# Delta rule: one sweep of nine steps for four heads, with copies over eight matrices, in place of two sweeps for two heads each

## The chip, the cores and the metric

The kernel runs on one core of a Trainium2 chip, in fp32. The metric is the device time of one execution in microseconds. Within the core TensorE does the matrix products, VectorE and ScalarE the elementwise work, GpSimd issues some of the transfers, and SyncE the weight loads. Each engine works through its own list of instructions in order; the order of each list is fixed when the kernel is built.

## The reference

One layer of a bidirectional hybrid block, for 256 tokens of width 2048:

```
mod  = silu(c) @ W_ada + b_ada          # six vectors: shift, scale, gate, twice
h    = RMSNorm(x) * (1 + scale) + shift
proj = h @ W_in                         # columns for the branches below
A    = bidirectional mLSTM, 4 heads (q, k 256 wide, v 512 wide)
B    = bidirectional gated delta rule, 16 heads of 128 (conv of 5 taps, SiLU, then the rule)
x    = x + gate * ((g_a * (A @ W_a) + g_b * (B @ W_b)) @ W_out)
x    = x + gate * SwiGLU(RMSNorm(x) * (1 + scale) + shift)
out  = RMSNorm(x)
```

The delta rule of one head and direction is S_t = a_t (I - b_t k_t k_t^T) S_{t-1} + b_t k_t v_t^T with o_t = S_t^T q_t. In chunks it needs the inverse T of a unit triangular matrix A = I + strict(b K K^T decay). With T known, a chunk takes a few products: T applied to the values, the correction between chunks, T applied again, and the output.

## The kernel before

**Products.** Weights come from memory in 1 MB tiles `raw`, are split by ScalarE into a high half (`wh`, a rounded copy) and by VectorE into a low half (`wl`, the remainder), and are multiplied in three products: high by high, high by low, low by high. `fjob` (L172 to L192) does one 128-column block of the input projection in two pieces of 24 matmuls of 256 columns; `tjob` (L198 to L274) does 512 columns in eight pieces of 12 matmuls of 512 columns. Both are generators: each `next` traces one piece. The tags `wh`, `wl` and `raw` have three buffers each.

**Filling.** `fills` is the list of projection jobs whose results go to memory for later: values, output gates, queries and keys of the mLSTM, merge gates. `fill(n)` traces n pieces of it. What is left of the list when the delta rule ends is emptied by `fill(1)`, `fill(2)` and `fill(1000)` at L1195 to L1205, among the first steps of the mLSTM.

**The delta rule.** The sixteen heads go in four groups of four (`GRP`). For a group:

- `gdn_phase1` (L639) prepares a head in two parts: decay matrices, the products of keys and queries, the matrices `cc`, `gg`, `at`, the values `vv` and the small factors `sm`. `gg`, `at`, `vv` and `cc` have six buffers (`NB`), so up to six heads are alive at once.
- `gdn_invert` (L747) inverts all 32 x 32 blocks of the four heads on VectorE, and `gdn_blocks` (L782) lays the inverses into `R`, `X` and `UL`.
- `gdn_phase2(g, p)` (L810), for p = 0 and 1, solves two heads, that is four matrices (two chunks by two heads), in nine steps. Steps 1 to 4 join the blocks to 64 and then 128 (matmuls `p1` to `p4` at L822, L831, L844, L856, with masked copies to `pt` at L823 and L845, a transposition at L834, and ScalarE copies to `X` and `UL`). Step 5 applies the inverse (`pa`), step 6 corrects between chunks (`pb`, `r` at L881), step 7 applies it again (`pc`), step 8 makes the output (`po`, L890 to L895) and squares it in `gdn_norm`, and step 9 scales it, transposes it (`px`, L902) and stores it (`obt`, L906 and L907).

**The order around it.** The loop at L1095 runs `gdn_phase2` step by step, and after step n traces `after[n]` (second pair `second[n]`, last group `last[n]`) pieces of `stream` (L948): first the projection jobs of two heads of the next group (twelve pieces, with the parts of `gdn_phase1` two and four pieces behind each head), then fills. A pair so gets 16 pieces in groups 0 to 2, that is 12 of the heads and 4 fills, and 13 fills in group 3.

**The modulation rows.** The matrix W_ada of the later four vectors is used row by row: `ask` loads one row tile of 1 MB and `add` (L120, the instruction at L125) multiplies it with silu(c) and sums it on VectorE. 48 rows are wanted before the feed-forward part, where `affn` (L1441) is made of them. `pump`, called once in each piece, asks for a row and adds it:

```
        if every[0] and count[0] % every[0] == 0:
            owed[0] = 1
        more = bool(unasked and every[0] and homes)
        if asked and owed[0] and asked[0][-1] > 2 and not held[0]:
            owed[0] = 0
            add()
        if more:
            ask()
```

There is one tile (`homes`) for a row until L1228, and two from there to L1440. `every` is 1 in the delta steps, 0 in the inversions and from L1192 to L1221, and 3 from L1229. `held` is true in steps 1 to 3 of each sweep, and no row is added then. At the fourth piece of the last output projection, L1437 to L1439, `sums` adds what is left.

**Order of the lists.** A planner orders each engine's list by the order of tracing and by when it expects inputs and buffers to be there. `order(...)` keeps an instruction behind the one traced before it on its engine, but does not hold later work back.

Of the kernel before, what the change touches and what calls it, by code (L numbers as in the profile page):

```python
# [15 lines left out]
P = 128  # L16
T = 256
# [35 lines left out]
def hybrid_block(ctx: ExitStack, tc: tile.TileContext, xr, nfr, crow, pk_d, cst_d, ada2, ada4, win0, winb, wint, wba, wbb, wo, wgu, wd, out, dbg=None):  # L53
# [693 lines left out]
    def gdn_invert(g):  # L747

        uu = uus.pop(g)
        tmp = bk.tile([64, 256], F32, tag="utmp", bufs=1, name=f"utmp{g}")  # L750
        cg = cgs[g] = bk.tile([P, 2, 4, P], F32, tag="z", bufs=1, name=f"cg{g}").rearrange("p k m c -> p k (m c)")
# [58 lines left out]
    def gdn_phase2(g, p):  # L810

        hd = [heads.pop(4 * g + 2 * p + e) for e in range(2)]
        te = [(t, e) for t in range(2) for e in range(2)]
        hs = slice(2 * p, 2 * p + 2)
        X4 = X.rearrange("p k (t h) q c -> p k t h q c", t=2)
        UL4 = UL.rearrange("p k (t h) c -> p k t h c", t=2)
        m4 = lambda a: a.rearrange("p (t h c) -> p t h c", t=2, h=2)

        p1 = gps(f"p1_{g}_{p}")
        pt0 = bk.tile([P, 4, P], F32, tag="pt", bufs=2, name=f"pt0_{g}_{p}")  # L820
        for i, (t, e) in enumerate(te):
            PE.matmul(p1[:, i * 32 : (i + 1) * 32], hd[e][0][:, 0, t], R[:, 0, 4 * t + 2 * p + e], start=True, stop=True)  # L822
        V.tensor_tensor(  # L823
            pt0.rearrange("p m (b c) -> p m b c", b=4),
            p1[:, 0:P].rearrange("p (m c) -> p m c", m=4).unsqueeze(2).broadcast_to([P, 4, 4, 32]),
            nxt.unsqueeze(1).unsqueeze(3).broadcast_to([P, 4, 4, 32]), ALU.mult,
        )
        yield
        p2 = gps(f"p2_{g}_{p}")
        for i, (t, e) in enumerate(te):  # L830
            PE.matmul(p2[:, i * 32 : (i + 1) * 32], pt0[:, i], R[:, 1, 4 * t + 2 * p + e], start=True, stop=True)  # L831
        E_ = p2[:, 0:P]
        Et = bk.tile([P, P], F32, tag="Et", bufs=1, name=f"Et{g}_{p}")
        V.transpose(Et, E_)  # L834
        S.activation(X4[32:64, 1, :, hs, 0], m4(E_[32:64]), AF.Copy)
        S.activation(X4[64:96, 1, :, hs, 1], m4(E_[64:96]), AF.Copy)
        S.activation(X4[32:64, 0, :, hs, 0], m4(Et[0:32]), AF.Copy)
        S.activation(X4[64:96, 0, :, hs, 1], m4(Et[96:128]), AF.Copy)
        yield

        p3 = gps(f"p3_{g}_{p}")
        pt1 = bk.tile([P, 4, P], F32, tag="pt", bufs=2, name=f"pt1_{g}_{p}")
        for i, (t, e) in enumerate(te):
            PE.matmul(p3[:, i * 64 : (i + 1) * 64], hd[e][0][:, 1, t], X[:, 0, 4 * t + 2 * p + e], start=True, stop=True)  # L844
        V.tensor_tensor(  # L845
            pt1.rearrange("p m (b c) -> p m b c", b=2),
            p3[:, 0 : 2 * P].rearrange("p (m c) -> p m c", m=4).unsqueeze(2).broadcast_to([P, 4, 2, 64]),
            half.unsqueeze(1).unsqueeze(3).broadcast_to([P, 4, 2, 64]), ALU.mult,
        )
        for b in range(4):  # L850
            c = 32 * (b ^ 1)
            S.activation(UL4[32 * b : 32 * b + 32, b % 2, :, hs, c : c + 32], m4(E_[32 * b : 32 * b + 32]), AF.Copy)
        yield
        p4 = gps(f"p4_{g}_{p}")
        for i, (t, e) in enumerate(te):
            PE.matmul(p4[:, i * 64 : (i + 1) * 64], pt1[:, i], X[:, 1, 4 * t + 2 * p + e], start=True, stop=True)  # L856
        S.activation(UL4[0:64, 0, :, hs, 64:128], m4(p4[0:64, 0 : 2 * P]), AF.Copy)
        V.tensor_copy(UL4[64:128, 1, :, hs, 0:64], m4(p4[64:128, 0 : 2 * P]))
        yield

        z = bk.tile([P, 2, 4, P], F32, tag="z", bufs=1, name=f"z{g}_{p}")
        r = bk.tile([P, 2, 2, P], F32, tag="r", bufs=1, name=f"r{g}_{p}")
        pair4 = lambda ps: ps.rearrange("p (e k c) -> p e k c", e=2, k=2)

        def apply(name, rhs, t0, t1):
            ps = pair4(gps(f"{name}_{g}_{p}"))
            for e in range(2):
                PE.matmul(ps[:, e, 0], UL4[:, 0, t0, 2 * p + e], rhs(e)[:, 0], start=True, stop=True)
                PE.matmul(ps[:, e, 1], UL4[:, 1, t1, 2 * p + e], rhs(e)[:, 1], start=True, stop=True)
            for e in range(2):  # L870
                sg3 = hd[e][5]
                S.activation(z[:, e, t0], ps[:, e, 0], AF.Copy, scale=sg3[:, t0, 0:1])
                S.activation(z[:, e, 2 + t1], ps[:, e, 1], AF.Copy, scale=sg3[:, t1, 1:2])

        apply("pa", lambda e: hd[e][3], 0, 1)
        yield
        pb = pair4(gps(f"pb_{g}_{p}"))
        for e in range(2):
            for i in range(2):
                PE.matmul(pb[:, e, i], hd[e][1][:, i], z[:, e, 3 * i], start=True, stop=True)  # L880
            V.tensor_tensor(r[:, e], hd[e][3][:, ::-1], pb[:, e], ALU.subtract)  # L881
        yield
        apply("pc", lambda e: r[:, e], 1, 0)
        yield
        po2 = gps(f"po_{g}_{p}")
        px = gps(f"px_{g}_{p}")
        for e in range(2):
            at, zz_ = hd[e][2], z[:, e]
# [10 lines left out]
        for e, on in enumerate(ons):  # L899
            h, hl_ = 4 * g + 2 * p + e, 2 * p + e  # L900
            for t in range(2):
                PE.transpose(px[:, (2 * e + t) * P : (2 * e + t + 1) * P], on[:, t], ident)  # L902
# [787 lines left out]
```

## Time and profile before

| what | value |
|---|---|
| median of three runs | 1951.5 us (1947.19 to 1954.09) |
| the profiled execution | 1949.33 us |
| its span, first to last instruction | 1947.5 us |
| TensorE busy (matmul) | 1919.7 us, 99% |
| VectorE busy | 1406.7 us, 72% |
| ScalarE busy | 1033.8 us, 53% |
| mean of the 16 DMA engines' traffic | 249 GB/s |
| four delta stages with both sweeps (groups 0 to 3) | 116.05, 115.39, 115.20, 90.70 us |

The profile names engines PE (matmul), PEld (weight load of TensorE), DVE (VectorE), ACT (ScalarE), POOL (GpSimd) and SP (SyncE). A row `p<-R,cc 128x32 f32 x8` is a group of instructions that write `p` from `R` and `cc`. An fp32 matmul appears as two records.

### The profile page before, as it was taken

What the parts mean: (1) busy time and instruction counts of PE and PEld (TensorE: products, weight loads), DVE (VectorE), ACT (ScalarE), POOL (GpSimd) and SP (SyncE); (2) the same over time, 40 slices, a digit from 0 to 9 for tenths busy, and PEclk for the clock granted to TensorE, in tenths of its full rate; (3) what the DMA queues carried; (4) which work ended last, traced back from release to release, by engine and by line L of the source; (5) the groups of instructions that cost most, each with busy time, mean ns of one, the idle gap of its engine ahead of it and who ended that gap; (6) DMA issues with size and microseconds to landing.
All of it is one profiled execution on the core that took longest, in us unless ns stands there. A gap on an engine that the chain in (4) does not pass through costs nothing.

```text
span 1947.5 us, 27217 instructions
## 1 busy us (share of the span) xinstructions
PE 1919.7 (99%) x10436; PEld 1699.3 (87%) x10436; DVE 1406.7 (72%) x2084; ACT 1033.8 (53%) x1564; POOL 124.1 (6%) x223
## 2 busy tenths in 40 slices
PE   8999999999999999999999999999999999999997
PEld 6888889998999899889788888888888888888886
DVE  6788886898788789876577988766666565555554
ACT  3147656775776587565544444644444444444443
POOL 0001220111011101120100000200000000000000
PEclk9999999999999999999999999999999999999999
DMA  9997676667676766686777998576667665655563
GB/s 399 420 358 236 188 256 249 214 224 238 219 220 204 241 220 238 208 293 245 268 289 266 351 353 314 195 263 245 246 239 260 239 219 199 204 207 209 196 208 137
DMA packets 80774, 485.68 MB, mean 249 GB/s; under 512 B 11434, under 2 KB 17138, under 8 KB 26626
## 3 DMA queue, kind: packets, MB, share of 16 engines
q1 hardware_dynamic: 64368, 451.02, 63.9%
q0 software_dynamic: 8672, 17.88, 4.3%
q10 hardware_dynamic: 7602, 15.03, 2.0%
q8 instruction: 82, 1.34, 0.3%
q14 instruction: 50, 0.40, 0.1%
HBM read 467.07 MB, written 16.82 MB: 248 GB/s over the span
## 4 chain that ended last, share of the span: by engine, by line
PE 90%; DMA 4%; DVE 3%; ACT 2%; issue 1%; SPq 0%; DVEq 0%; ACTq 0%
PE acc_up L247 4%; PE acc_up L249 4%; PE acc_up L248 4%; PE acc_gt L248 4%; PE acc_d L248 4%; PE acc_gt L249 4%; PE acc_d L247 4%; PE acc_d L249 4%; PE acc_gt L247 4%; DMA ra<-ada 3%; PE acc_b L186 3%; PE acc_o L247 3%; PE acc_o L248 3%; PE acc_o L249 3%; PE acc_b L188 3%; PE acc_b L187 3%
## 5 line engine op out<-in xcount | busy, mean ns | idle before, releaser
L215 DVE TENSOR_TENSOR wl_d<-raw_d,wh_d 128x1024 fp32r<-128x1024 f32 x88 | 107.7, 1225 | 105.9 <-ACT wh_d L213 105.9
L215 DVE TENSOR_TENSOR wl_up<-raw_up,wh_up 128x1024 fp32r<-128x1024 f32 x88 | 107.7, 1225 | 100.7 <-ACT wh_up L213 100.7
L215 DVE TENSOR_TENSOR wl_gt<-raw_gt,wh_gt 128x1024 fp32r<-128x1024 f32 x88 | 107.7, 1224 | 78.6 <-ACT wh_gt L213 78.6
L186 PE MATMUL acc_b<-hh,wh_b 128*128 128x256 f32 x576 | 161.9, 281 | 0.0
L213 ACT ACTIVATE wh_d<-raw_d 128x1024 fp32r<-128x1024 f32 x88 | 92.9, 1056 | 126.5 <-PE acc_d L248 117.7
L188 PE MATMUL acc_b<-hh,wl_b 128*128 128x256 f32 x576 | 158.7, 276 | 0.0
L187 PE MATMUL acc_b<-hl,wh_b 128*128 128x256 f32 x576 | 158.3, 275 | 0.0
L213 ACT ACTIVATE wh_gt<-raw_gt 128x1024 fp32r<-128x1024 f32 x88 | 92.8, 1055 | 117.1 <-PE acc_gt L248 71.1
L213 ACT ACTIVATE wh_up<-raw_up 128x1024 fp32r<-128x1024 f32 x88 | 92.7, 1055 | 108.1 <-PE acc_up L248 77.1
L125 DVE SCALAR_TENSOR_TENSOR ada<-ada,crow 128x2048 f32<-128x2048 f32 x64 | 146.2, 2284 | 0.0
L247 PE MATMUL acc_up<-wh_up,hfh 128*128 128x512 f32 x352 | 133.4, 379 | 0.0
L248 PE MATMUL acc_up<-wh_up,hfl 128*128 128x512 f32 x352 | 133.4, 379 | 0.0
L249 PE MATMUL acc_up<-wl_up,hfh 128*128 128x512 f32 x352 | 133.4, 379 | 0.0
L247 PE MATMUL acc_gt<-wh_gt,hfh 128*128 128x512 f32 x344 | 131.6, 383 | 0.0
L248 PE MATMUL acc_gt<-wh_gt,hfl 128*128 128x512 f32 x344 | 131.3, 382 | 0.2 <-DVE hfl L1475 0.2
L247 PE MATMUL acc_d<-wh_d,ffh 128*128 128x512 f32 x344 | 130.5, 379 | 0.0
L248 PE MATMUL acc_d<-wh_d,ffl 128*128 128x512 f32 x344 | 130.5, 379 | 0.0
L249 PE MATMUL acc_gt<-wl_gt,hfh 128*128 128x512 f32 x344 | 130.4, 379 | 0.0
L249 PE MATMUL acc_d<-wl_d,ffh 128*128 128x512 f32 x344 | 130.4, 379 | 0.0
L595 PE MATMUL first<-x,raw 128*128 128x256 f32 x488 | 110.1, 386 | 6.0 <-ACT x L587 6.0
L595 PEld LDWEIGHTS first<-x,raw 128*128 128x128 f32 x488 | 92.9, 192 | 23.3 <-ACT x L587 10.7
L187 PEld LDWEIGHTS acc_b<-hl,wh_b 128*128 128x128 f32 x576 | 110.6, 192 | 0.1
(403 smaller groups left out, 5294.7 us busy)
## 6 DMA issues: line engine op xcount, KB each, us to landing
ada<-ada SPq DMA_DIRECT2D x64, 1024.0 KB, 5.2
raw_gt<-wgu SPq DMA_DIRECT2D x44, 1024.0 KB, 5.0
raw_up<-wgu SPq DMA_DIRECT2D x44, 1024.0 KB, 5.0
raw_d<-wd SPq DMA_DIRECT2D x44, 1024.0 KB, 4.9
raw_b<-winb SPq DMA_DIRECT2D x36, 1024.0 KB, 5.6
ra<-ada SPq DMA_DIRECT2D x30, 1025.0 KB, 14.9
raw_z<-wint SPq DMA_DIRECT2D x16, 1024.0 KB, 5.0
raw_v<-wint SPq DMA_DIRECT2D x16, 1024.0 KB, 5.4
```

Source lines behind the costliest of these rows:

```text
L125: order(V.scalar_tensor_tensor(raw, raw, 1.0, row_c[:, :D], ALU.mult, ALU.mult, accum_out=mod[:, c : c + 1]))
L186: PE.matmul(o, wh[:, k], woven(hh[:, kk]), start=kk == 0, stop=False)
L187: PE.matmul(o, wh[:, k], woven(hl[:, kk]), start=False, stop=False)
L188: PE.matmul(o, wl[:, k], woven(hh[:, kk]), start=False, stop=kk == KB - 1)
L213: order(S.activation(wh, raws[u][:, k0 : k0 + 2], AF.Copy), early)
L215: order(V.tensor_tensor(wl, raws[u][:, k0 : k0 + 2], wh.bitcast(F32), ALU.subtract), early or beside[0])
L247: order(PE.matmul(ps[t], xh[:, kk, c], woven(wh[:, k]), start=kk == 0, stop=False), early and steps > 1)
L248: PE.matmul(ps[t], xl[:, kk, c], woven(wh[:, k]), start=False, stop=False)
L249: PE.matmul(ps[t], xh[:, kk, c], woven(wl[:, k]), start=False, stop=kk == last)
L595: PE.matmul(first[o], raw[:, o], x[:, b], start=b == 0 and o % 2 == 0, stop=b == KB - 1 and o % 2 == 1)
```

## The change

`gdn_phase2(g, p)` becomes `gdn_solve(g)`: the same nine steps run once in a group, over four heads and eight matrices. Each masked copy, transposition and block copy takes eight matrices in one instruction; products that need 512 columns for four matrices now use two PSUM banks (`pa`, `pb`, `pc`, `po`, `px`). The buffers change: `pt` is one tile of eight matrices in place of two of four, shared by `pt0`, `pt1`, `r` and `on`; `z` grows from two heads to four; `Et` shares the tile of the inversion's `utmp`. All the small matmuls are kept in their order. The scaling of the output is in two parts, each run at a later piece.

`stream` brings the four heads of the next group in one go (24 pieces), and the tables of pieces are new: 28 in groups 0 to 2 (24 and 4 fills; 32 with 8 fills before), 26 in group 3 as before. `held` covers steps 1 to 3 of one sweep, which have 8 pieces (7 in group 3).

```diff
-    def gdn_phase2(g, p):
...
+    def gdn_solve(g):
+
+        hd = [heads.pop(4 * g + h) for h in range(GRP)]
+        th = [(t, h) for t in range(2) for h in range(GRP)]
+        m8 = lambda a: a.rearrange("p (m c) -> p m c", m=8)
+        turned_ = lambda name: bk.tile([P, 8, P], F32, tag="pt", bufs=1, name=f"{name}_{g}")
+
+        p1 = gps(f"p1_{g}")
+        pt0 = turned_("pt0")
+        for m, (t, h) in enumerate(th):
+            order(PE.matmul(p1[:, m * 32 : (m + 1) * 32], hd[h][0][:, 0, t], R[:, 0, m], start=True, stop=True), m)
         V.tensor_tensor(
             pt0.rearrange("p m (b c) -> p m b c", b=4),
...
+            m8(p1[:, 0 : 2 * P]).unsqueeze(2).broadcast_to([P, 8, 4, 32]),
+            nxt.unsqueeze(1).unsqueeze(3).broadcast_to([P, 8, 4, 32]), ALU.mult,
         )
         yield
...
+        Et = bk.tile([P, 2 * P], F32, tag="utmp", bufs=1, name=f"Et{g}")
         V.transpose(Et, E_)
...
+        S.activation(X[32:64, 1, :, 0], m8(E_[32:64]), AF.Copy)
+        S.activation(X[64:96, 1, :, 1], m8(E_[64:96]), AF.Copy)
+        S.activation(X[32:64, 0, :, 0], m8(Et[0:32]), AF.Copy)
+        S.activation(X[64:96, 0, :, 1], m8(Et[96:128]), AF.Copy)
+        yield
...
+        S.activation(UL[0:64, 0, :, 64:128], m8(p4[0:64]), AF.Copy)
+        V.tensor_copy(UL[64:128, 1, :, 0:64], m8(p4[64:128]))
+        yield
+
+        z = bk.tile([P, GRP, 4, P], F32, tag="z", bufs=1, name=f"z{g}")
+        by_bank = lambda name: [gps(f"{name}{i}_{g}").rearrange("p (e k c) -> p e k c", e=2, k=2) for i in range(2)]
...
+        apply("pa", lambda h: hd[h][3], 0, 1)
+        yield
+        r = turned_("r").rearrange("p (h k) c -> p h k c", h=GRP)
+        pb = by_bank("pb")
...
+        apply("pc", lambda h: r[:, h], 1, 0)
+        yield
+        pos = [gps(f"po{i}_{g}") for i in range(2)]
...
+        on = turned_("on").rearrange("p (h t) c -> p h t c", h=GRP)
+        gdn_norm(g, on, pos, [hd[h][4][:, 2:4] for h in range(GRP)])
         yield
         settle(only="scaled")
+        settle(only="scaled")
+        px = [gps(f"px{i}_{g}") for i in range(2)]
...
+            obt = obp.tile([P, T], F32, tag="obt", bufs=2, name=f"obt{4 * g + h}")
...
-        for h in range(h0, min(h0 + 2, NH_B)):
+        for h in range(h0, min(h0 + GRP, NH_B)):
...
-    after = (0, 1, 2, 1, 2, 2, 2, 2, 4, 0)
-    last = (0, 1, 2, 1, 2, 2, 1, 1, 3, 0)
-    second = (0, 2, 2, 1, 2, 2, 2, 2, 3, 0)
+    after = (0, 2, 3, 3, 3, 4, 4, 4, 5, 0)
+    last = (0, 2, 3, 2, 3, 4, 3, 3, 6, 0)
...
+        pieces = stream(4 * g + 4)
+        for n in range(1, 10):
+
+            held[0] = n < 4
+            next(blocks, None)
+            next(solve, None)
+            if g == 3 and n in (5, 7):
+                next(first2[n // 7])
+            for _ in range((last if g == 3 else after)[n]):
+                next(pieces)
```

184 lines of the change are left out of this document (75 added, 109 removed).

## The prediction

> **What bounds the kernel.** I read the page first: busy time of the engines, then the chain of work that ended last.
>
> ```profile
> span 1947.5 us, 27217 instructions
> PE 1919.7 (99%) x10436; PEld 1699.3 (87%) x10436; DVE 1406.7 (72%) x2084; ACT 1033.8 (53%) x1564; POOL 124.1 (6%) x223
> PE 90%; DMA 4%; DVE 3%; ACT 2%; issue 1%; SPq 0%; DVEq 0%; ACTq 0%
> ```
>
> TensorE is busy for 99% of the span and makes 90% of the chain. The change removes no matmul, so it can only move the time in which TensorE waits. How much of that lies in the delta stages is read from the busy time in stretches of time, one from the first `p1` of each group to its last `px`, and one for the output projections:
>
> ```profile
> 315.08:431.13 116.05, 114.55 (x906) 110.32 (x904) 99.56 (x197) 87.57 (x177) 10.59 (x21) 1.00 0.66 219
> 496.53:611.92 115.39, 114.40 (x931) 111.10 (x929) 99.51 (x197) 86.44 (x179) 10.48 (x21) 1.00 0.67 223
> 674.16:789.36 115.20, 114.89 (x977) 112.74 (x976) 101.33 (x201) 89.28 (x181) 9.75 (x19) 1.00 0.67 226
> 853.08:943.78 90.70, 90.70 (x594) 83.77 (x593) 61.56 (x87) 49.02 (x97) 0.53 (x1) 1.00 0.70 252
> 1155.07:1232.99 77.92, 77.92 (x382) 68.74 (x380) 64.13 (x69) 38.27 (x51) 0.00 (x0) 1.00 0.83 313
> ```
>
> The columns are elapsed time, then busy time of PE, PEld, DVE, ACT, POOL. TensorE is idle for 1.50 + 0.99 + 0.31 + 0.00 = 2.80 us in the four stages together, at a granted clock of 1.00. VectorE is at 86% there (99.51 of 115.39) and ScalarE at 75%, so both are near a limit of their own. What the weight loads of TensorE waited for, from 310 to 945 us:
>
> ```profile
> PEld acc_z L249 <- DVE wl_z L215: 2.5, 2, 1.3
> PEld vps L666 <- ACT vf L354: 1.5, 3, 1.0
> PEld acc_a L188 <- DVE wl_a L183: 1.4, 1, 1.4
> PEld p L831 <- DVE pt L823: 1.4, 1, 1.4
> PEld pb L880 <- DVE r L881: 1.2, 3, 0.4
> PEld p L856 <- DVE pt L845: 0.4, 2, 0.2
> ```
>
> The sweep's own steps wait 1.4 + 1.2 + 0.4 = 3.0 us. The `vps` wait (1.5) belongs to the first part of `gdn_phase1`, and the `acc_z` and `acc_a` waits (3.9) to the inversions between the stages.
>
> **The change part by part.**
>
> *Small matmuls joined.* How a batch stands among the pieces:
>
> ```profile
> 315.08 0.97 PE L822 MATMUL p<-R,cc 128*128 128x32 f32 x8
> 315.89 0.36 PE L186 MATMUL acc_b<-hh,wh_b 128*128 128x256 f32 x1
> 318.65 0.98 PE L831 MATMUL p<-R,pt 128*128 128x32 f32 x8
> 319.47 0.36 PE L186 MATMUL acc_b<-hh,wh_b 128*128 128x256 f32 x1
> ```
>
> A batch of eight records takes 0.81 us (315.08 to 315.89), a piece of 24 takes 2.76 (315.89 to 318.65): 0.101 and 0.115 us a record. The batch is already as dense as its surroundings, so twice the batch costs twice the time. A border between the two kinds could cost up to the 0.115 of one record; nine borders fewer in each of four groups bound this at 0 to 4.1 us gained. I take 0.
>
> *Cover of each step.* Before, one or two pieces (2.76 to 5.5 us) lay behind a step; now two to five (5.5 to 13.8). The waits of 3.0 us at `p` and `pb` should go. Bounds: nothing gained, or all of 3.0 and the 1.5 at `vps` with it. I take 3.0: a `vps` part stands two pieces behind its head as before. What is late next is the split half of a piece, that is VectorE.
>
> *Copies over eight matrices.* From the groups by line, VectorE and then ScalarE, in group 1:
>
> ```profile
> L183 DVE TENSOR_TENSOR wl_b<-raw_b,wh_b 128x1024 fp32r<-128x1024 f32 x22 | 26.8, 1217 | 5.2 <-ACT wh_b L181 5.1
> L351 DVE SCALAR_TENSOR_TENSOR cv<-pad,pk,cv 128x256 f32<-128x256 f32 x48 | 23.0, 479 | 1.3 <-ACT cv L349 0.8
> L823 DVE TENSOR_TENSOR pt<-p,cst 128x512 f32<-128x512 f32 x2 | 1.3, 672 | 1.4 <-PE p L822 1.4
> L799 ACT ACTIVATE X<-cg 32x256 f32<-32x256 f32 x4 | 1.7, 414 | 0.4 <-ACT ev_a L375 0.4
> L835 ACT ACTIVATE X<-p 32x128 f32<-32x128 f32 x2 | 0.5, 270 | 0.6 <-DVE Et L834 0.6
> ```
>
> A masked copy of 128x1024 is bounded by the split of that size, 1.22 us, against 2 x 0.67: 0.12 saved, four copies become two, so 0.24 a group. A 32x256 copy takes 0.41 against 2 x 0.27: 0.13 saved, eight times a group (four of `X`, four of `UL`), 1.0 us of ScalarE. Both engines have idle time, so the sum gets 0; should they bind, it is some 1.2 us a group. The wait for one copy grows by 1.22 - 0.67 = 0.55 us; it is hidden by at least two pieces, and would cost 1.1 a group (two masked copies) or 4 us in all without them.
>
> [...]
>
> *Fewer fills beside the heads.* In groups 0 to 2 the sweep has 28 pieces, not 32; the four fills, 12 in all, run after the last sweep. On TensorE this is nothing: 12 pieces of 2.6 to 2.8 us are moved. On VectorE the first 24 pieces get denser: 24 splits at 1.217 (29.2), 48 taps of the convolution (23.0), four row sums (9.2, below), and about three quarters of the rest of group 1. That rest is 99.5 - 32 x 1.217 - 23.0 - 13.75 = 23.8, three quarters 17.9. Sum 79.3 us. TensorE has 24 x 2.76 = 66 us of pieces and three quarters of what is no piece, 115.4 - 1.0 - 32 x 2.7 = 28, so 21: 87 us. VectorE at 91% keeps up, with 8 us to spare in 24 pieces. I take 0; the other end is below with the rivals.
>
> *Row sums.* `pump` adds a row every fourth piece outside `held`. Before, pieces 1 to 4 of the first pair and 1 to 5 of the second were held, which gives adds at 5, 9, 13 and 22, 26, 30: six a group. After, eight are held, adds at 9, 13, 17, 21, 25: five (group 3: 8, 12, 16, 20, 24, five). The row sums alone, in the same stretches (each counts twice, with a read of its accumulator):
>
> ```profile
> 496.53:611.92 115.39, 13.75 (x12) 1.00 0.67 223
> 853.08:943.78 90.70, 13.76 (x12) 1.00 0.70 252
> 943.78:1061.87 118.09, 11.47 (x10) 0.99 0.77 280
> 1061.87:1212.00 150.13, 43.56 (x38) 1.00 0.90 345
> ```
>
> Six a group it is, 24 in four, then 5 and 19: 48. The change leaves four more for the end, and the places there are taken, one every third piece. VectorE before the feed-forward part, the first row being the last sum of all:
>
> ```profile
> 1203.99 2.28 DVE L125 SCALAR_TENSOR_TENSOR ada<-ada,crow 128x2048 f32<-128x2048 f32 x1
> 1207.54 0.18 DVE L1441 SCALAR_TENSOR_TENSOR affn<-mod,pk 128x16 f32<-128x16 f32 x1
> 1211.76 1.28 DVE L1285 TENSOR_TENSOR tmss<-acc_o,gm 128x512 f32<-128x512 f32 x2
> 1212.96 1.28 DVE L1288 TENSOR_TENSOR x<-x,tmss 128x512 f32<-128x512 f32 x2
> 1218.44 1.23 DVE L215 TENSOR_TENSOR wl_o<-raw_o,wh_o 128x1024 fp32r<-128x1024 f32 x1 [0.79 <-ACT wh_o L213]
> 1233.60 0.40 DVE L1368 TENSOR_SCALAR hf<-pxn,affn,mod 128x128 f32<-128x128 f32 x1
> ```
>
> and TensorE's need of the split of 1218.44:
>
> ```profile
> 1222.93 0.38 PE L249 MATMUL acc_o<-wl_o,mgh 128*128 128x512 f32 x1
> ```
>
> After the change one more add falls at the second piece of the last output projection, and `sums` traces three at its fourth. From 1211.76 VectorE then has the residual (2.4), an add (2.2), the splits of two pieces and one for the gate (3 x 1.14 where they follow each other), and two adds (4.4) before the split of the fifth piece (1.14): 13.6, ending at 1225.4. It is needed at 1222.9, so TensorE waits 2.5 us. The last row is asked for when the first of the two homes is free, near 1222; its transfer lands 5.2 us later:
>
> ```profile
> ada<-ada SPq DMA_DIRECT2D x64, 1024.0 KB, 5.2
> ob_d<-obt ACTq DMA_DIRECT2D x16, 128.0 KB, 2.6
> ```
>
> That add ends near 1230 and pushes the last split by about 0.5. `affn` is then made near 1231 and not at 1207.5; its reader at 1233.6 is shifted by 3 as well. So 3.0 us lost. Bounds: 0, if the planner puts the splits ahead of the sums; 4 x 2.28 + 5.2 = 14.3, if all sums and the wait are exposed.
>
> *Stores.* `obt` has two buffers, and four stores now follow each other: ScalarE waits for the third some 2.6 us (second row above). Behind it stand the high halves of the inversion's first pieces, which run up to three buffers ahead. 0; without that cover 2.6 x 4 = 10.
>
> *Buffers of `at`.* The third head of the next group takes the buffer that the first head of this group frees at `po`. Its turn is piece 22, `po` stands behind piece 23, so these copies wait one to two pieces, with the two `ks` banks. The planner can put the splits ahead of them: 0. If VectorE stands in its list instead, up to 4 us a group (1.5 pieces of 2.76), 12 in three.
>
> Sum against the profiled execution of 1949.33 us (span 1947.5): -3.0 + 3.0 = 0, so 1949.3. The profiled execution is 2.2 below the median; against the median, 1951.5.
>
> **The rivals.**
>
> *Faster: the sums are hidden and the sweep is free of waits.* The planner takes the splits first (0 in place of 3.0), and 3.0, 1.5 and a part of the borders, 2, come back: -6.5, 1945. For it: VectorE had idle time between 1204 and 1229 (the splits there follow waits for ScalarE). Against it: the sums are traced ahead of the splits.
>
> *Slower: the sums at the end are exposed.* Place: the last output projection. There TensorE has no idle time at all (77.92 of 77.92), so each us by which VectorE is late is lost. It decides when the split leads its need by less than the 2.3 of one sum; the row above leads by 3.4 (1219.6 to 1222.9). With 4 x 2.28 = 9.1 exposed and 3.0 regained: +6.1, and up to 11.3 with the transfer; 1960.
>
> *Slower: VectorE bounds the sweep*, by the wait for `at` or by the denser heads. The point is a lead of three split buffers, about 8 us. At 4 us a group, 12 - 3.0 + 3.0 = 12: 1963. For it: 91% busy; against it: pieces can go ahead in the list.
>
> *A little slower: the first matmul of a step waits for the whole copy.* Place: `p2` behind `pt0`, `p4` behind `pt1`. 1.1 us a group, 4 in all: 1955.5, inside the bound of no change. It decides when the cover falls under the copy and the split ahead of it, 2.4 us; the least cover is 5.5. [...]
>
> **How the numbers follow.** Forecast (between 1945.7 and 1957.3, the bound of 0.3% or 5.85 us, about what a measurement of this kernel can tell from no change): 0.45, and the late copies 0.05, which end there too: no change 0.5. Faster rival 0.2. Exposed sums 0.18, VectorE in the sweep 0.12: slower 0.3. The range from 1944.5 to 1961 leaves out half of the faster case's lower tail and most of the last: 2 in 10.
>
> **What would show it.** Right: the `p` and `pb` rows gone from the waits; four stages of 105, 105, 105 and 90 us (115.4 - 4 x 2.6); ten row-sum records a stage; `affn` after 1225 and a wait of about 2.5 us at the fifth piece of the last output projection. Wrong: waits of `acc_b` for `wl_b` in the sweep, VectorE standing before `at`, or ScalarE before `obt`.

## The result and the profile after

| | before | after |
|---|---|---|
| median | 1951.12 us (1947.19 to 1954.09) | 1977.41 us (1975.97 to 1978.41) |
| profiled execution, its span | 1949.33 us, 1947.5 us | 1976.56 us, 1974.8 us |
| mean granted TensorE clock | 0.997 | 0.991 |

The changed kernel is slower: ratio 1.0136, 95% interval 1.0122 to 1.0150, that is 26.3 us. The forecast was no change, with a range to 1961. The head of the page of after and its chain of work that ended last:

```profile
span 1974.8 us, 27160 instructions
PE 1931.4 (98%) x10436; PEld 1709.7 (87%) x10436; DVE 1401.9 (71%) x2060; ACT 1034.7 (52%) x1532; POOL 124.2 (6%) x223
PE 77%; DVE 10%; DMA 6%; ACT 5%; issue 2%; POOL 0%; ACTq 0%; DVEq 0%; SPq 0%
```

The number of matmuls is unchanged. TensorE is "busy" 11.7 us longer with the same work, which is the first hint that its clock was lower; its share of the chain falls from 90% to 77%, VectorE's rises from 3% to 10%. Busy time by stretches, one for each stage from its first `p1` to its last `px` (elapsed, then PE, PEld, DVE, ACT, POOL, the granted clock, DMA):

```profile
314.87:424.17 109.30, 106.08 (x857) 102.70 (x855) 89.80 (x185) 82.08 (x166) 10.59 (x21) 0.98 0.61 199
492.23:603.97 111.74, 108.07 (x907) 106.43 (x906) 92.11 (x188) 83.75 (x172) 10.48 (x21) 0.97 0.62 202
666.49:775.77 109.28, 106.08 (x857) 102.70 (x855) 90.51 (x186) 82.05 (x166) 9.75 (x19) 0.98 0.59 204
845.54:935.60 90.06, 90.06 (x547) 82.57 (x546) 58.30 (x82) 47.24 (x85) 0.53 (x1) 1.00 0.67 244
```

TensorE idles 3.22 + 3.67 + 3.20 us in the first three stages and not at all in the fourth, which has no heads beside it. And the clock is 0.97 to 0.98 there, where it was 1.00 before. What TensorE's weight loads waited for, 314 to 945 us:

```profile
PEld vps L666 <- ACT vf L354: 7.0, 6, 1.4
PEld acc_z L247 <- ACT wh_z L213: 5.7, 3, 2.3
PEld acc_ma L249 <- DVE wl_ma L215: 3.1, 1, 3.1
PEld acc_b L188 <- DVE wl_b L183: 3.0, 6, 0.8
PEld acc_z L249 <- DVE wl_z L215: 2.5, 4, 1.3
PEld acc_a L188 <- DVE wl_a L183: 1.9, 2, 1.3
PEld acc_mb L249 <- DVE wl_mb L215: 1.3, 2, 1.0
PEld acc_o L249 <- DVE wl_o L215: 1.0, 1, 1.0
```

The `p` and `pb` rows of before are gone. In their place stand the transpose of a head's values (`vps`, 1.5 before), the first half of the next output gate's weights (`wh_z`, not in the list before), and late split halves (`wl`) in more places.

**Where the 27 us of span lie.** For every matmul record I took the distance to the start of the next one, less the lower quartile of that distance for its kind; differences under 0.05 us count as nothing. Between 310 and 1270 us this lost time is 25.4 us before and 49.3 after (what is taken as one kind moves each total by some 2 us): outside the stretches at half clock 23.7 before and 37.4 after, inside them 1.7 and 11.9. The remaining 3 us I can't place. Summed over groups 0 to 2, with the stretches at half clock in it, by the time since the group's first `p1` ("later" ends at the next group's):

```
us after p1      0-20  20-40  40-60  60-80  80-100  100-120  later   sum
before            1.2    2.8    2.1    1.2     3.5      0.7    3.9  15.3
after             3.4    8.0    5.8    0.7     0.2     14.3    4.0  36.4
```

Two places carry the loss: 20 to 60 us behind `p1`, and the end of the sweep. The first place, in group 0, on ScalarE and with one row of VectorE:

```profile
325.22 1.68 ACT L799 ACTIVATE X<-cg 32x256 f32<-32x256 f32 x4
...
328.55 1.28 ACT L354 ACT_TABLE_LOAD   x1
329.85 0.42 ACT L354 ACTIVATE kq<-cv 128x256 f32<-128x256 f32 x1
330.27 0.76 ACT L850 ACTIVATE UL<-p 32x256 f32<-32x256 f32 x2
331.06 0.38 ACT L346 ACTIVATE pad<-acc_b 128x256 f32<-128x256 f32 x1
331.47 0.38 ACT L850 ACTIVATE UL<-p 32x256 f32<-32x256 f32 x1
331.87 0.51 ACT L349 ACTIVATE cv<-pad,pk 128x256 f32<-128x256 f32 x1
332.41 1.00 DVE L351 SCALAR_TENSOR_TENSOR cv<-pad,pk,cv 128x256 f32<-128x256 f32 x2 [4.97 <-ACT cv L349]
```

ScalarE runs from 324.4 to 335.2 without a pause: block copies, `X` and `UL` copies, a table load, and only then the eviction `pad` and the first tap `cv` of a head. VectorE stands for 4.97 us at that `cv`, with split halves behind it in its list; their high halves, too, come out of ScalarE only from 332.28 on, after the same row of copies. In the same list of before the longest wait for `cv` in this stretch is 0.33 us. The second place, the end of the same sweep, on ScalarE and then TensorE:

```profile
413.33 1.28 ACT L368 ACT_TABLE_LOAD   x1
415.24 1.28 ACT L354 ACT_TABLE_LOAD   x1
416.96 1.28 ACT L368 ACT_TABLE_LOAD   x1
418.87 1.28 ACT L678 ACT_TABLE_LOAD   x1
423.77 0.84 ACT L908 ACTIVATE obt<-px,pk 128x256 f32<-128x256 f32 x2 [2.68 <-PE px L904]
425.13 1.06 ACT L213 ACTIVATE wh_z<-raw_z 128x1024 fp32r<-128x1024 f32 x1 [0.52 <-ACT obt L908]
426.24 0.48 PE L247 MATMUL acc_z<-wh_z,hh 128*128 128x512 f32 x1 [2.07 <-ACT wh_z L213]
```

The norms of four heads, the last head's preparation and the evictions meet here. `wh_z` stands behind `obt` in ScalarE's list, `obt` waits for `px`, and `px` runs on TensorE behind the last head's `ks`. TensorE then has nothing left but `acc_z`, and waits 2.07 us.

**The clock.** Three stretches of 3.41 us each, one after the other; in the first TensorE waits for `vf`:

```profile
343.06:346.48 3.42, 3.00 (x27) 3.00 (x28) 3.39 (x3) 3.39 (x6) 0.00 (x0) 1.00 0.01 2
346.48:349.89 3.41, 3.41 (x18) 3.41 (x18) 3.38 (x6) 1.20 (x4) 0.00 (x0) 0.50 0.62 187
349.89:353.30 3.41, 3.41 (x32) 3.41 (x32) 2.22 (x5) 1.06 (x1) 0.00 (x0) 1.00 0.97 401
```

The clock column is 0.50 in the middle one, and 18 records lie in it against 32 in the next. Between 300 and 1275 us there is one such window before and seven after: six more at 1.7 us make 10 us, the whole part "inside" above.

### The profile page after: what moved, and what is told of

Read it like the earlier page. It is cut to its first block, busy times and chain, and to the rows that moved or that the text cites. A ratio compares the mean times of both kernels' runs of the same rounds, so it can differ in the third digit from the quotient of the medians.

```text
span 1974.8 us, 27160 instructions
## 1 busy us (share of the span) xinstructions
PE 1931.4 (98%) x10436; PEld 1709.7 (87%) x10436; DVE 1401.9 (71%) x2060; ACT 1034.7 (52%) x1532; POOL 124.2 (6%) x223
## 4 chain that ended last, share of the span: by engine, by line
PE 77%; DVE 10%; DMA 6%; ACT 5%; issue 2%; POOL 0%; ACTq 0%; DVEq 0%; SPq 0%
PE acc_up L247 4%; PE acc_up L248 4%; PE acc_up L249 4%; PE acc_gt L248 4%; PE acc_d L248 4%; PE acc_d L247 4%; PE acc_d L249 4%; PE acc_gt L249 4%; PE acc_gt L247 4%; DMA ra<-ada 3%; PE acc_o L249 2%; PE first L595 2%; PE acc_o L248 2%; PE acc_o L247 2%; DVE cv L351 2%
## 5 line engine op out<-in xcount | busy, mean ns | idle before, releaser
L188 PEld LDWEIGHTS acc_b<-hh,wl_b 128*128 128x128 f32 x576 | 112.8, 196 | 3.0 <-DVE wl_b L183 3.0
```

The lines of the kernel that those rows point to most:

```text
L188: PE.matmul(o, wl[:, k], woven(hh[:, kk]), start=False, stop=kk == KB - 1)
```

## Experiments

The changed kernel unless said otherwise. Ratios are to the kernel before, run beside each.

**The stream of pieces, both ways round.** First the joined sweep with the old stream:

```diff
-        for h in range(h0, min(h0 + GRP, NH_B)):
+        for h in range(h0, min(h0 + 2, NH_B)):
...
+        if more:
+            yield from more
...
-    after = (0, 2, 3, 3, 3, 4, 4, 4, 5, 0)
+    after = (0, 2, 3, 3, 3, 4, 5, 5, 7, 0)
...
-        pieces = stream(4 * g + 4)
+        pieces = stream(4 * g + 4, stream(4 * g + 6, None) if g < 3 else None)
```

> The changed kernel with 32 pieces beside each sweep, as before: heads 4g+4 and 4g+5 are followed by four fills, and heads 4g+6 and 4g+7 by four more (table 2,3,3,3,4,5,5,7). The joined steps and the copies over eight matrices stay. Theory DENSITY (24 pieces of heads in a row keep ScalarE and VectorE late, and the four fills in their midst let them catch up): most of the 26 us comes back, 1951 to 1960, and the waits of vps for vf fall from 7.0 us towards the 1.5 of before. Theory BURST (the copies of nine steps come in bursts on ScalarE in steps 2 to 4 and at the end, whatever lies between): 1970 to 1978, vps waits and the wait of 2.2 us before z stay. Theory ROW SUMS (those left to the end cost it): 1973 to 1977, since as many row sums stay per sweep plus at most one.

Measured 1982.33 us, ratio 1.0159 (1.0142 to 1.0176); `vps` waits 8.0 us in seven places. It lies above every range that was expected: four fills in the midst of the heads don't help. DENSITY, as a cause by itself, falls. Then the old pairs with the new stream:

```diff
-        for h in range(h0, min(h0 + 2, NH_B)):
+        for h in range(h0, min(h0 + GRP, NH_B)):
...
-    after = (0, 1, 2, 1, 2, 2, 2, 2, 4, 0)
+    after = (0, 1, 2, 1, 2, 2, 2, 2, 2, 0)
...
-    second = (0, 2, 2, 1, 2, 2, 2, 2, 3, 0)
+    second = (0, 2, 2, 1, 2, 2, 1, 1, 3, 0)
...
-            pieces = stream(4 * g + 2 * p + 4)
+            if not p:
+                pieces = stream(4 * g + 4)
...
```

> The kernel before with its two pairs in turn and its copies over four matrices, but with the one stream of four heads and 28 pieces (24 of heads, then 4 fills) that the changed kernel has. DENSITY: slower than before by most of the 26 us, 1968 to 1977, with waits for vf and for halves of weights between the second and the last head. BURST: as before, 1950 to 1955, for only the cover of the p and pb steps changes by a piece or two. ROW SUMS: 1955 to 1960 if five or fewer are made per sweep.

Measured 1957.58 us, 1.0039 (1.0024 to 1.0054): some 8 of the 26 us at most belong to the stream. `vps` waits 1.4 us, as before. The time lies in the range of ROW SUMS, but its condition is not met: six sums a sweep are made, as before.

**The end of the sweep.**

```diff
+            if n == 9 and g < 3:
+                zj = z_job(g + 1, 2)
+                next(zj)
...
-            fills.insert(0, z_job(g + 1))
+            fills.insert(0, zj)
```

> The changed kernel, in which the first two halves of the weights of the next output gate (wh_z, wl_z) are asked for ahead of the turned outputs' step, so that ScalarE has wh_z in front of obt in its list. Theory TAIL (wh_z behind obt at the sweep's end costs 5.7 us of waits in three groups, and brings the granted clock to half for 3.41 us after some of them): acc_z no longer waits for wh_z, 1966 to 1971. DENSITY and BURST: the wait is moved to something else (px or ks late), 1972 to 1978.

Measured 1974.25 us, 1.0123 (1.0107 to 1.0138), which overlaps the changed kernel's interval. The wait for `wh_z` falls from 5.7 to 2.3 us, and the one for `wl_z` rises from 2.5 to 7.5: most of it moved from ScalarE to VectorE, as the second expectation had it.

**VectorE's load.**

```diff
+        n = D // 8 if thin[0] else D
-        order(V.scalar_tensor_tensor(raw, raw, 1.0, row_c[:, :D], ALU.mult, ALU.mult, accum_out=mod[:, c : c + 1]))
+        order(V.scalar_tensor_tensor(raw[:, :n], raw[:, :n], 1.0, row_c[:, :n], ALU.mult, ALU.mult, accum_out=mod[:, c : c + 1]))
...
+            thin[0] = n < 9
...
```

> The changed kernel, in which the row sums made inside the four sweeps read an eighth of each row (so a part of the modulation is left out; about 2.3 us of VectorE become about 0.4 for each of five per sweep, some 10 us of VectorE per sweep). Theory VECTORE (it cannot keep up with 24 pieces of heads): most of the loss goes, 1951 to 1960. Theory SCALARE (its list is late, VectorE waits for it): little changes, 1972 to 1978, and VectorE's waits for cv of ScalarE grow.

Measured 1964.98 us, 1.0082 (1.0057 to 1.0106): about 10 us back, between the two expectations. By the table of lost time the end of the sweep falls from 14.3 to 5.7 and 40 to 60 us from 5.8 to 1.3, while 20 to 40 us keeps its 8.0. The lighter sums leave a part of the modulation out, so this run is a test and no version to use. VectorE's load is a part of the loss, and not in the first place.

**The block copies, the size of copies, later preparations.**

```diff
+        for _ in blocks:
+            pass
         solve = gdn_solve(g)
```

> The changed kernel, in which the 16 block copies of a group (X and UL out of cg, 12 on ScalarE of 0.41 us and 4 on VectorE of 0.29 us) are all asked for ahead of the first step instead of one set of four with each of the steps 1 to 4. Theory BURST (in steps 2 to 4 ScalarE has the four block copies, the eight of the steps, a table load and the evictions of the heads in one row, so the convolutions and then vf of the first heads are late): the waits of vps for vf fall from 7.0 us in six places to under 3, and 1977 becomes 1964 to 1971. Theory VECTORE (the late work is VectorE's own: sums, splits and convolutions): 1974 to 1979, vf as late as before.

Measured 1975.71 us, 1.0125 (1.0101 to 1.0149); `vps` waits 7.5 us. The four block copies have left the burst shown above, and `vf` is late all the same: a row sum of 2.28 us now lies among the taps of its convolution (341.30 to 343.58).

```diff
-        for b in range(4):
-            c = 32 * (b ^ 1)
-            S.activation(UL[32 * b : 32 * b + 32, b % 2, :, c : c + 32], m8(E_[32 * b : 32 * b + 32]), AF.Copy)
+        for k in (slice(0, 4), slice(4, 8)):
+            for b in range(4):
+                c = 32 * (b ^ 1)
+                S.activation(UL[32 * b : 32 * b + 32, b % 2, k, c : c + 32], m8(E_[32 * b : 32 * b + 32])[:, k], AF.Copy)
...
```

> The changed kernel, in which every copy over eight matrices (X, pt, UL) is made in two over four, as before, while the nine joined steps stay: 22 more instructions per group, about 1.2 us more ScalarE and 0.3 us more VectorE. If the size of the copies costs something (the next matmuls wait for all eight matrices): 1965 to 1972. If it is as forecast (nothing): 1975 to 1982.

Measured 1974.45 us, 1.0119 (1.0103 to 1.0135): not told apart from the changed kernel.

```diff
-            todo += [[2, h], [4, h]]
+            todo += [[3, h], [5, h]]
```

> The changed kernel, in which the two parts of a head's preparation come three and five pieces behind its last product in place of two and four. Theory LATE VF (the first part's transpose waits 7.0 us in six places because vf is not ready two pieces after): these waits go, and some of the half clocks behind them, 1966 to 1971; the last head's parts come one piece later, so the sweep needs a 29th piece. Theory THROUGHPUT (VectorE and ScalarE have too much in these stretches): the wait moves to the halves of weights (wl_b) or to z, 1974 to 1979.

Measured 1967.84 us, 1.0085 (1.0069 to 1.0102): 10 us back. The wait for `vf` only falls to 5.0 us, and `wl_b` rises from 3.0 to 7.3; the lost time at 20 to 40 us falls from 8.0 to 1.2, but at 60 to 80 us it rises from 0.7 to 5.8, so that the three groups together go from 36.4 to 31.7 only. The half-clock windows go from seven to four.

The edits of e3, e5 and e7 together:

```diff
-            todo += [[2, h], [4, h]]
+            todo += [[3, h], [5, h]]
...
+        for _ in blocks:
+            pass
...
+                zj = z_job(g + 1, 2)
+                next(zj)
...
```

> The changed kernel with three of these edits at once: block copies ahead of the first step, preparations one piece later, and the weights of the next output gate asked for ahead of the turned outputs. If the waits for vf, for the first half of z and the burst are separate causes: the sum of their gains, 1955 to 1963. If VectorE's load in the sweep is the common cause, the waits move to halves of weights and it stays at 1970 to 1977.

Measured 1972.46 us, 1.0126 (1.0092 to 1.0159). Their gains don't add; the waits of `acc_b` for `wl_b` are 9.7 us.

**The hold of the row sums.**

```diff
-            held[0] = n < 4
+            held[0] = n < 2
```

> The changed kernel, in which row sums are held back only during step 1 (2 pieces) of a sweep instead of steps 1 to 3 (8 pieces). Theory SPREAD (VectorE is busy 7.0 and 11.5 of 15 us in the first two stretches of a sweep, while the sums are held, and then 15.0 and 15.0 of 15 us, where heads and sums wait for each other): six or seven sums per sweep, VectorE under 14.5 of 15 us in each stretch, fewer waits for vf and halves of weights, 1960 to 1970. Theory IN THE WAY (a sum of 2.3 us in steps 2 and 3 stands in front of Et and pt, and the p matmuls and convolutions wait for it): 1976 to 1985.

Measured 1975.88 us, 1.0136 (1.0121 to 1.0152): no change. Seven sums a sweep instead of five are made, the waits move, and there are nine half-clock windows. The same hold put into the kernel before:

```diff
-                held[0] = n < 4
+                held[0] = not p and n < 6
```

> The kernel before, in which row sums are held back as in the changed one: during the first 8 pieces of the first pair's sweep, and not at all in the second's. Everything else as before. SPREAD: the sums come closer together beside the later heads, some of them one per group fewer, 1955 to 1965. If the hold is not the cause: 1949 to 1953.

Measured 1957.22 us, 1.0034 (1.0023 to 1.0045), and `vps` waits 6.1 us in six places. The place of the sums alone is worth 7 us there, with the same wait and with four half-clock windows in the profiled execution, where the kernel before has one. Short hold, later preparations and early `wh_z` together:

```diff
-            todo += [[2, h], [4, h]]
+            todo += [[3, h], [5, h]]
...
-            held[0] = n < 4
+            held[0] = n < 2
...
+                zj = z_job(g + 1, 2)
+                next(zj)
...
```

> The changed kernel with the short hold, preparations one piece later, and the weights of the next output gate asked for ahead of the turned outputs. SPREAD with late vf and the tail as separate costs: 1952 to 1962. If VectorE's total in the sweep, not its spread, is the limit: 1965 to 1975. Faster than the kernel before (under 1948) would need the joined sweep to cost nothing at all, and neither theory gives that.

Measured 1970.27 us, 1.0101 (1.0085 to 1.0117), in the range of the branch in which VectorE's total is the limit (e14 below speaks against that branch).

**Joined, staggered, in turn.** Here the order of the sweep's steps changes. Stream, 28 pieces (here in group 3 too, where the changed kernel has 26) and the buffers' total sizes are the changed kernel's; steps that are not joined are those for two heads, with copies over four matrices. First each step for pair 0 and, half of the step's pieces later, for pair 1:

```diff
+    staggered = (0, 2, 3, 3, 3, 4, 4, 4, 5, 0)
...
+            for p in range(2):
+                next(pairs[p], None)
...
+                for _ in range((staggered[n] + p) // 2 if n < 9 else 0):
+                    next(pieces)
...
```

> One sweep for a group with the changed kernel's 28 pieces, hold of the sums and buffers, but each of the nine steps is made in two halves, pair 0's, then after half of the step's pieces pair 1's, with copies over four matrices. Light and heavy steps lie where the changed kernel has them; only the joining of the step for four heads is undone. Theory JOINED (a step's work for four heads comes at once on ScalarE and VectorE and stands in front of the heads' chain): 1955 to 1960, as the two pairs in turn with the one stream (1957.6). Theory ORDER (all light steps first, all heavy ones last, beside the last heads): 1970 to 1977.

Measured 1975.62 us, 1.0134 (1.0107 to 1.0161): as slow as joined. Then steps 1 to 4 of pair 0, of pair 1, steps 5 to 9 of pair 0, of pair 1 (pair, step, pieces behind it):

```diff
+    light_first = (
+        (0, 1, 1), (0, 2, 2), (0, 3, 1), (0, 4, 2), (1, 1, 1), (1, 2, 1), (1, 3, 2), (1, 4, 1),
+        (0, 5, 2), (0, 6, 2), (0, 7, 2), (0, 8, 2), (0, 9, 1), (1, 5, 2), (1, 6, 2), (1, 7, 2), (1, 8, 2), (1, 9, 0),
+    )
...
```

> The steps of two heads each, with copies over four matrices, in this order: steps 1 to 4 of pair 0, steps 1 to 4 of pair 1, steps 5 to 9 of pair 0, steps 5 to 9 of pair 1, beside the changed kernel's 28 pieces and with its hold of the sums. Nothing is joined, but all light steps (little for VectorE) come first and all heavy ones last. JOINED: 1955 to 1960. ORDER: 1968 to 1977. The control is the two pairs in turn with the same stream, 1957.6.

Measured 1953.35 us, 1.0012 (1.0003 to 1.0021). Both theories fall: JOINED said that staggering would do, ORDER that this would not. The longest waits of the staggered sweep and then of this one, 310 to 945 us:

```profile
PEld vps L666 <- ACT vf L354: 10.4, 9, 1.8
PEld acc_z L247 <- ACT wh_z L213: 5.8, 3, 2.3
...
```

```profile
...
PEld pb L880 <- issue: 3.3, 4, 1.0
PEld vps L666 <- ACT vf L354: 2.9, 6, 0.7
PEld acc_ma L249 <- DVE wl_ma L215: 1.1, 1, 1.1
PEld acc_a L188 <- DVE wl_a L183: 0.4, 1, 0.4
...
```

With the pairs in turn `vf` is late by half a us on average, and `wh_z` has no row; what the `pb` row waited for, the profile does not show. VectorE is busy for 82.58 us there from 330 to 420 us, against 80.61 in the joined sweep, so its total is not the limit by itself. Staggered and with 32 pieces, against e13:

```diff
-    staggered = (0, 2, 3, 3, 3, 4, 4, 4, 5, 0)
+    staggered = (0, 2, 4, 3, 4, 4, 4, 4, 7, 0)
...
-        pieces = stream(4 * g + 4)
+        pieces = stream(4 * g + 4, stream(4 * g + 6, None) if g < 3 else None)
```

> The staggered sweep with 32 pieces in the order of before (four fills behind the second and behind the fourth head). JOINED: 1948 to 1953, as before. ORDER: 1970 to 1983, as the joined sweep with 32 pieces (1982).

Measured 1979.04 us, 1.0149 (1.0134 to 1.0165), as the joined sweep with 32. Now one half of the sweep at a time. Steps 1 to 4 joined, 5 to 9 in turn:

```diff
+    plan = [(0, m, 1) for m in (2, 3, 3, 3)] + [(1, m, 0) for m in (2, 2, 2, 2, 1)] + [(2, m, 0) for m in (2, 2, 2, 2, 0)]
...
+        gens = [gdn_light(g)] + [gdn_heavy2(g, p) for p in range(2)]
...
```

> The changed kernel with steps 1 to 4 joined for four heads as it has them (2,3,3,3 pieces), but with steps 5 to 9 made for pair 0 (2,2,2,2,1 pieces) and then for pair 1 (2,2,2,2,0). Per 20 us behind a group's first p matmul, summed over three groups, TensorE lost in the changed kernel 8.0 us (20 to 40), 5.8 (40 to 60) and 14.3 (100 to 120), and in the order that nothing joins (e14) 2.3, 4.8 and 0.2. Theory HEAVY STEPS (four heads' norms, gates and stores meet the last head's preparation at the end): the 14.3 goes, the 8.0 stays, with its half clocks 1958 to 1965. Theory LIGHT STEPS (what is late comes from the joined steps 1 to 4): 1970 to 1978.

Measured 1963.03 us, 1.0066 (1.0051 to 1.0081). And steps 1 to 4 in turn, 5 to 9 joined:

```diff
+    plan = [(0, m, 1) for m in (1, 2, 1, 2)] + [(1, m, 0) for m in (1, 1, 2, 1)] + [(2, m, 0) for m in (4, 4, 4, 5, 0)]
...
+        gens = [gdn_light2(g, p) for p in range(2)] + [gdn_heavy(g)]
...
```

> The reverse: steps 1 to 4 for pair 0 and then for pair 1 with copies over four matrices, as in e14, and steps 5 to 9 joined for four heads as in the changed kernel (4,4,4,5,0 pieces). HEAVY STEPS: the 14.3 us at 100 to 120 stay and the 8.0 at 20 to 40 fall to 2 to 3, 1964 to 1972. LIGHT STEPS: 1952 to 1958.

Measured 1967.46 us, 1.0081 (1.0064 to 1.0098). Both times lie in the ranges of HEAVY STEPS. The waits of these two, 310 to 945 us, heavy steps in turn and then light steps in turn:

```profile
PEld vps L666 <- ACT vf L354: 4.5, 6, 1.0
...
PEld acc_b L188 <- DVE wl_b L183: 2.4, 3, 0.8
...
PEld acc_z L249 <- DVE wl_z L215: 1.1, 2, 0.6
...
```

```profile
PEld acc_z L247 <- ACT wh_z L213: 4.6, 2, 2.3
PEld vps L666 <- ACT vf L354: 2.9, 6, 0.5
PEld acc_b L188 <- DVE wl_b L183: 2.4, 3, 0.8
...
```

With the heavy steps in turn the wait for `wh_z` is gone and the one for `vf` falls to 4.5 us only; with the light steps in turn `vf` is as little late as in e14 and `wh_z` still is. The lost time of these kernels, worked out as above:

```
us after p1      0-20  20-40  40-60  60-80  80-100  100-120  later   sum   ratio
joined            3.4    8.0    5.8    0.7     0.2     14.3    4.0  36.4  1.0136
staggered         3.5    6.9    5.7    2.5     2.1     14.1    1.3  36.2  1.0134
light in turn     1.0    2.3   10.0    1.0     3.4     11.0    1.8  30.5  1.0081
heavy in turn     3.4    4.8    5.5    1.8     3.3      0.5    4.7  23.9  1.0066
both in turn      1.0    2.3    4.8    2.1     2.5      0.2    1.5  14.5  1.0012
```

The heavy steps in turn are worth 0.70% from the joined sweep and 0.69% from the one with light steps in turn; the light steps in turn 0.55% and 0.54%. The two add up to 24 of the 26 us. The ratios are over four executions or more; the rows of lost time are of one each, for heavy in turn the fastest of its four (1959.65 us), for light in turn the slowest (1969.11). Without the stretches at half clock they add up in the same way: 28.7 us joined, 21.1 with the light and 22.2 with the heavy steps in turn, 14.5 with both. The loss is shown to lie in how the steps of two pairs stand to each other: it comes when the same kind of step runs for all four heads within one stretch of the heads' pieces, at once or a piece or two apart. The size of the copies, the products over two banks and the single tile `pt` of the joined sweep are not needed for it: e13 has none of them and is as slow.

**Two last ones.** Thin row sums with later preparations and early `wh_z`:

```diff
...
-            todo += [[2, h], [4, h]]
+            todo += [[3, h], [5, h]]
...
+            thin[0] = n < 9
...
+                zj = z_job(g + 1, 2)
+                next(zj)
...
```

> The changed kernel with row sums in the sweep that read an eighth of each row (a part of the modulation is left out), preparations one piece later and the weights of the next output gate asked for early: the three edits that gave 10.5, 10 and 2.5 us alone. If they are separate costs: 1952 to 1956. If they are three faces of one lateness: 1958 to 1965.

Measured 1953.89 us, 1.0017 (1.0008 to 1.0026). The single gains of 0.54, 0.51 and 0.13% add up to 1.18, and 1.19% is measured: with VectorE lighter they add, where in e8 and e11, with its full load, they did not. And the best order, tuned, against e14:

```diff
-            todo += [[2, h], [4, h]]
+            todo += [[3, h], [5, h]]
...
-            held[0] = n < 5 and (p == 0 or n < 3)
+            held[0] = n < 4 and p == 0
```

> The order of e14 (1953.4), with row sums held back only in the first 4 pieces instead of 8, and a head's preparation one piece later. In e14 five sums per sweep leave three more to the last output projection than before, which costs about 3 us there, and vps waits 2.9 us for vf. If both are given back: 1946 to 1951, level with the kernel before or a little under it. If the hold protects the light steps: 1955 to 1962.

Measured 1960.67 us, 1.0057 (1.0042 to 1.0072): slower than e14, in the range given for a hold that protects the light steps. Which of the two edits does the harm is not shown; the later preparation alone helped the joined sweep (e5). No version here beats the kernel before; e14 comes closest.

## Why the prediction was wrong

*Joining the steps: the term that is missing.* The sum took the joining as a gain, 3.0 us of cover, and the copies over eight matrices as 0. It had no term for what equal steps of four heads, run close together, do to the heads' chains that stand in the same lists. This is the step that failed. With the same stream of pieces, taking the joining apart in both halves (e14) brings back 24 of the 26 us; the heavy steps alone are worth some 14 (e17) and the light ones some 11 (e18).

*Fewer fills beside the heads: failed, by its method.* The step set 79.3 us of VectorE work against 87 us of TensorE and said that VectorE keeps up. The totals were about right and decide nothing. Busy time from 330 to 420 us, its first stretch and the sum, before and then after:

```profile
330.00:345.00 15.00, 14.78 (x132) 14.59 (x132) 14.21 (x23) 14.13 (x28) 0.00 (x0) 1.00 0.55 200
...
sum 90.00, PE 88.50 PEld 85.49 DVE 80.73 ACT 71.91 POOL 10.07; mean PE 14.75 PEld 14.25 DVE 13.45 ACT 11.99 POOL 1.68
```

```profile
330.00:345.00 15.00, 13.62 (x120) 13.24 (x120) 11.50 (x19) 12.88 (x24) 0.00 (x0) 1.00 0.42 141
...
sum 90.00, PE 86.79 PEld 84.10 DVE 80.61 ACT 71.74 POOL 10.59; mean PE 14.46 PEld 14.02 DVE 13.43 ACT 11.96 POOL 1.77
```

VectorE and ScalarE do the same work in the 90 us (80.73 and 80.61, 71.91 and 71.74), and TensorE idles 1.7 us more. What differs is when it is done: from 330 to 345 us VectorE works 11.50 us against 14.21 before, since it stands for the first 2.4 us at the `cv` shown above, and TensorE works 13.62 us against 14.78. The lead of each operand shows the lateness: from 315 to 940 us the split halves of the weights were ready less than 0.1 us ahead of TensorE 5 times of 193 before, 16 of 183 after and 2 of 188 in e14 (from the end of each split to the first matmul record that reads it). The count does not price a kernel: e16 has 16 of 188, at 1.0017. The fewer fills, with whatever else these two kernels change, cost 2 us (e14, which also moves four row sums) to 8 us (e2), by the order of the steps.

*Cover of each step: half right.* The `p` and `pb` waits went, as foretold. But "a `vps` part stands two pieces behind its head as before" was taken to mean that its wait stays at 1.5 us. The place stayed; the chain in front of it (eviction, first tap, four taps, SiLU, over two engines) got the joined light steps between its links, and the wait became 7.0. e18, which takes only these apart, brings it to 2.9.

*Stores: failed in its cover.* ScalarE does stand before `obt`, though hardly for the store: from 314 to 900 us its waits for `ob_d` are 0.4 us, once, and those for `px` 5.9 us. The step said that the inversion's first halves "run up to three buffers ahead". They do not: `wh_z` stands behind `obt`, and TensorE waits 5.7 us for it. e17, with only two heads' norms and stores at the end, has none of this wait.

*Row sums: right.* Five a stage, and more at the end: ten records a stage, and in the last output projection of after, on VectorE and on TensorE:

```profile
492.23:603.97 111.74, 11.47 (x10) 0.97 0.62 202
845.54:935.60 90.06, 11.46 (x10) 1.00 0.67 244
```

```profile
1244.86 2.29 DVE L125 SCALAR_TENSOR_TENSOR ada<-ada,crow 128x2048 f32<-128x2048 f32 x1
...
1247.07 1.22 DVE L215 TENSOR_TENSOR wl_o<-raw_o,wh_o 128x1024 fp32r<-128x1024 f32 x1
1248.34 0.70 PE L249 MATMUL acc_o<-wl_o,mgh 128*128 128x512 f32 x2 [1.73 <-DVE wl_o L215]
1255.16 0.17 DVE L1444 SCALAR_TENSOR_TENSOR affn<-mod,pk 128x16 f32<-128x16 f32 x1
```

The wait is 1.73 us where 2.5 was forecast, and `affn` is made 6.3 us ahead of the first gate product (1261.4), where it had 26.9 us before. From the mLSTM's first product to there the kernel takes 1.2 us more (323.30 - 290.62, less the 12 fills of 2.62 us), while the lost time, worked out as above, grows by 3.8 us, from 7.8 to 11.6; the 3.0 forecast lies between the two, and what makes them differ is not shown. Behind the waits there a half-clock window begins at 1261.3 us, where the profile of before has none: another 1.7 us, and whether it belongs to the row sums is not shown.

*Small matmuls and copies: right.* Sixteen `p` records take 1.70 us (eight took 0.81). The copies in halves (e4) change nothing that can be measured. In the second stage TensorE idles 3.67 us with VectorE at 82% busy (92.11 of 111.74), and neither e4 nor the staggered e13, which both make the copies over four matrices, takes the loss away (1974.45 us in e4, where the changed kernel has 1977.41; 36.2 us of lost time in e13, 36.4 in the changed kernel).

*Buffers of `at`.* VectorE does not stand before these copies. Whether the third head's late buffer adds to the end of the sweep stays open, since e17 frees the buffer earlier too.

*The stages and the rivals.* 105, 105, 105 and 90 us were foretold; 109.3, 111.7, 109.3 and 90.1 came. Of the rivals, "VectorE bounds the sweep" names the right place, with a chance of 0.12 and 1963 us. Its sign, `acc_b` waiting for `wl_b`, is there (0.2 before, 3.0 after), but its two mechanisms are not the ones shown, and it stops 14 us short. Of the 27 us between the profiled executions, 10 are the clock, which the prediction read as 1.00 and took for given.

What stays open: which single instruction is late is different in each kernel, and I can't say why a distance of one or two pieces between the pairs' equal steps does not help while one of six to nine does.

## What to carry to other kernels

A mean busy share, even over one stage, doesn't tell whether an engine keeps up; ask how far ahead of its need each operand is ready, and what stands in the in-order lists of the two engines that make it. Steps of independent groups of work that run in turn are a spread of load: joining them saves instructions and can cost more than it saves, and the loss can be priced by putting one half of the steps back at a time. Where TensorE is the bound, count its short waits once as waits and, as a further risk, by the stretches at half clock that went with them here (10 of the 27 us).

## What the runs showed of the hardware

Short waits go with half clock. Over the traces of all these kernels, from 310 to 1270 us, the time at full clock is cut into windows of 3.41 us, the length of each stretch at half clock: where TensorE lost less than 0.3 us in a window, 37 of 4855 were followed by a window at half clock; at 1.2 to 2.1 us, 18 of 125; above 2.1 us, 18 of 38. So most waits have no such window behind them, and not every window has a wait ahead of it: of the 84 windows at half clock, 20 follow on no wait above 0.25 us in the 14 us ahead. In the trace of after the starts of its seven (346.48, 428.40, 523.98, 595.66, 698.06, 940.40 and 1261.26 us) lie 24, 28, 21, 30, 71 and 94 times 3.413 us apart. The longest single gap in the 14 us ahead of the seven windows of after is 2.24 us. The one at 940.4 us, and the one before at 1009.7, are of those with no wait above 0.25 us there.

In one kernel the clock also tells the spread between executions. The one with light steps in turn gave 1962.15 us at a mean clock of 0.996, 1966.50 at 0.994, and 1968.42 and 1969.11 at 0.992: 0.004 of 1967 us is 7.9 us, and the times differ by 7.0. The changed kernel does not show this: 1975.97 us at 0.991 and 1978.41 at 0.992.
